# Up projection: the halo's low halves move into the first term, sixteen matmuls of 256 columns follow each other, and the hand-over into the projection is put in another order

## The chip, the cores and the metric

The kernel runs on one core of one Trainium2 chip. Its time is the device time of one execution in microseconds (us). Three runs of the kernel before gave 1258.06, 1258.51 and 1260.97 us; the median is 1258.51. The engines are named as in the profile: PE (TensorE: matmuls, and PEld for the loads of their stationary operand), DVE (VectorE), ACT (ScalarE), POOL (GpSimd) and SP (SyncE, which here issues most DMAs).

## The reference, cut to what matters

The kernel computes one layer of a decoder on 1024 tokens and 16 prepended meta tokens, all in float32: a normalised input, a first projection, a convolution branch and an attention branch that are gated and merged, an output projection with a residual and a layer norm, and then a ConvFFN. The change lies in the up half of that ConvFFN and at the hand-over into it:

```
D_MODEL = 1024
SEQ = 1024
D_FF = 2816
FFN_TAPS = 3

def hybrid_layer(...):
    ...
    h = layer_norm(DEEPNORM_ALPHA * h + mixed @ w_out, ln1_g, ln1_b)
    up = causal_dwconv(h @ ffn_w_up, ffn_dw, ffn_dw_b)
    u, g = jnp.split(up, 2, axis=-1)
    f = (jax.nn.gelu(g, approximate=False) * u) @ ffn_w_down
    return layer_norm(DEEPNORM_ALPHA * h + f, ln2_g, ln2_b)
```

`h @ ffn_w_up` is a product of 1026 rows (1024 tokens and two before them, which the causal convolution of three taps needs) with a matrix of 1024 x 5632.

## The kernel before

**Precision.** A float32 operand x is kept as two rounded parts, hi = round(x) and lo = round(x - hi). A product a x b is then three matmuls, a_hi b_hi + a_hi b_lo + a_lo b_hi, which accumulate in PSUM. The weights are the stationary side (`ah`, `al`), the tokens the moving side.

**Seven products for eight.** The up projection is cut into 22 chunks. For each, a 2 x 2 arrangement of blocks (the two halves of the features of h, by the two halves of the tokens; the two halves of the outputs) is computed by seven block products in place of eight. In the order of the loop they are named `B11`, `B21`, `BT2`, `BT4`, `BT1`, `BT3`, `B22` after their token operand. `B11`, `B21` and `B22` are blocks of h itself, the four `BT` are differences of such blocks, formed on DVE (`form_t2`, `form_t3`, `form_t4`). The weight side of each product is a raw block or a sum of raw blocks, formed per chunk on DVE (L1411), rounded to its high half on ACT (L1393) and subtracted to its low half on DVE (L1394). These halves lie in a ring of ten places, so they are made ahead of use.

**Columns.** A half of the tokens has 514 columns: 2 of halo (the two tokens ahead of it) and 512. It is cut into two parts, part 0 with 258 columns (halo and 256) and part 1 with 256. Each product goes over 4 blocks of 128 features with 3 terms: 12 matmuls of 258 columns for part 0, and then 12 of 256 columns for part 1, in the order features outside, terms inside (L1572). Part 0 ends at the end of one PSUM bank, part 1 begins the next.

**PSUM.** Four tiles of two banks each are used in turn: X (`px`), Z (`pz`), V4 (`pw`) and Y (`py`). The products go to X, Z, X, V4, Y, X, Y. Between them ACT copies X and Y out (`copy`, L1584) and DVE combines (`tt`, L1580) into the four blocks c11, c21, c22, c12. For each of those, `conv_ffn` does the three taps: the first on ACT (L1499), two more on DVE (L1500, L1501); gelu runs on ACT (L1505), gate times value on DVE (L1509), and the result goes to DRAM.

**The hand-over.** Ahead of the up projection stands the output projection (`out_rows`: PSUM tiles `ps_w`, added to the residual on DVE in L1327, normalised in L1351), one block of 128 tokens after another, the last of them block 5. Its rows have to be transposed on PE (`turn`, L1361) and scaled on ACT (L1374) before the operands of part 0 can be formed. For this reason chunk 0 goes in two passes: part 1 first, and after its third product the transposes of block 5, in the banks of V4 and Z; then part 0. While part 1 runs, DVE and ACT make the operands of part 0: `form_t2` and the others (L1273), high halves on ACT (L1264), low halves on DVE (L1269).

**What sets the order.** The loop is written in the order above. A scheduler then puts each engine's instructions into one fixed row, by rank and by the orders that `after` adds; `line` chains the DVE work of the hand-over one behind the other in the order of the text. On the chip each engine takes its row in order and waits for semaphores. The lines that matter below:

```
        if pinned_w[0]:
            line(ins)
        elif ring_next[0] <= 10:
            after(ins, formed[0])
...
                    for k in range(4):
                        ks = slice(k * P, (k + 1) * P)
                        for j, (x, hl) in enumerate(((ah, 0), (ah, 1), (al, 0))):
                            ins = nc.tensor.matmul(o, x[:, ks], bmat(sub, q, hl, k), ...)
```

Of the kernel before, what the change touches and what calls it, by code (L numbers as in the profile page):

```python
# [58 lines left out]

HW = 514  # L60
SUB = [(0, 258), (258, HW)]

W_LEN = 2304

# [48 lines left out]
def tile_hybrid_layer(  # L113
# [1113 lines left out]
    def quadrant(sub, kk, h):  # L1227
        i = h * KC + kk * 4
        return FA[:, h1_at(sub, i):h1_at(sub, i + 4)]

    B_AT = [[(RHC, 40), (RHO, 4096 + 40)] + [(OA, OA_UP + i * KC * BS[0]) for i in range(4)] + [(RX, 56)],
            [(OC, OC_UP + i * 2048) for i in range(4)] + [(RHC, 4096 + R_DN), (RHC, 2048 + R_DN), (RHC, 6144 + R_DN)]]
    B11, B21, BT2, BT1, BT3, BT4, B22 = range(7)

    def bsum(sub, q, hl):
        n, s = SUB[sub][1] - SUB[sub][0], BS[sub]
        t, o = B_AT[sub][q]
        return t[:, o + hl * 4 * s:o + (hl + 1) * 4 * s].rearrange("p (k n) -> p k n", k=4)[:, :, :n]

    def bmat(sub, q, hl, k):  # L1240
        return bsum(sub, q, hl)[:, k]

    lined, high = [], []

# [14 lines left out]

    def bsplit(sub, q, src, cs=slice(None)):  # L1260
        with rank(RK_SUMS):
            hi, lo = (bsum(sub, q, hl)[:, :, cs] for hl in range(2))
            src = wide(src)[:, :, cs]
            ins = nc.scalar.copy(hi, src)  # L1264
# [4 lines left out]
            line(nc.vector.tensor_tensor(lo, src, f32(hi), OP.subtract))  # L1269

    def bsub(out, x, y, cs=slice(None)):
        with rank(RK_SUMS):
# [83 lines left out]
    def turn(i, r, n, ins, banks=None, behind=None, upper=False):  # L1356
        with rank(RK_TURN):
            for j, k0 in enumerate((4, 0) if upper else (0, 4)):
                ps = banks[j] if banks else pat.tile([P, 512], F, name="ps_h", tag="s", bufs=2)
                for k in range(4):  # L1360
                    ins = nc.tensor.transpose(ps[:, k * P:(k + 1) * P], r[:, (k0 + k) * P:(k0 + k + 1) * P], ident)  # L1361
                    if behind:
                        after(ins, behind[-1])
                        behind.append(ins)
                for k in range(k0, k0 + 4):
                    src = ps[:, (k - k0) * P:(k - k0) * P + n]
                    if n < P:
                        dst = edge[:, 0, k]
                    else:
                        h, jj = divmod(i, 4)  # L1370
                        sub = 0 if jj < 2 else 1
                        a = 2 + jj * P - SUB[sub][0]
                        dst = h1F(sub, h, k)[:, a:a + P]
                    nc.scalar.activation(dst, src, AF.Identity, bias=b1col(k), scale=g1col(k))  # L1374
# [10 lines left out]
    def wsplit(src):  # L1385
        i = ring_next[0]
        ring_next[0] += 1
        i %= len(RING)
        if RING[i] is None:
            RING[i:i + 2] = wsp_flat()  # L1390
        t = RING[i]
        hi, lo = t[:, 0:512], t[:, 512:1024]
        nc.scalar.copy(hi, src)  # L1393
        ins = nc.vector.tensor_tensor(lo, src, f32(hi), OP.subtract)  # L1394
        if pinned_w[0]:
            line(ins)
        elif ring_next[0] <= 10:
            after(ins, formed[0])
        return hi, lo

    def w_rows(c):
# [89 lines left out]
        ft_next[0] += 1  # L1491
        return FA[:, i * 512:(i + 1) * 512]

    c11, c21, u2 = (FA[:, 4128 + i * HW:4128 + (i + 1) * HW] for i in range(3))
    c12, c22, u13 = (RT[:, i * HW:(i + 1) * HW] for i in range(3))

    def conv_ffn(cc, o):
        t = ftmp()
        nc.scalar.activation(t, cc[:, 2:HW], AF.Identity, bias=ffw(3, o), scale=ffw(2, o))  # L1499
        nc.vector.scalar_tensor_tensor(t, cc[:, 1:HW - 1], ffw(1, o), t, OP.mult, OP.add)  # L1500
        nc.vector.scalar_tensor_tensor(t, cc[:, 0:HW - 2], ffw(0, o), t, OP.mult, OP.add)  # L1501
        return t
# [42 lines left out]
            load((td if i < FH else sd)[j, :, h * 1024:(h + 1) * 1024], t[h])  # L1545

    last_mm, copied = [], []
    w_first(7)
    pinned_w[0] = False
    for c in range(FC):  # L1550
        V4, X, Z, Y = (pup.tile([P, 1024], F, name=n, tag=n) for n in ("pw", "px", "pz", "py"))
        passes = ((1,), (0,)) if c == 0 else ((0, 1),)
        for subs in passes:
            last = subs == passes[-1]
            w_next = iter(range(7))
            a, b = SUB[subs[0]][0], SUB[subs[-1]][1]

            def at(t):
                return t[:, 254 + a:254 + b]

            def prod(q, bank, first):
                if last:
# [2 lines left out]
                else:  # L1565
                    ah, al = w_ready[next(w_next)]
                for sub in subs:
                    o = bank[:, 254 + SUB[sub][0]:254 + SUB[sub][1]]
                    for k in range(4):
                        ks = slice(k * P, (k + 1) * P)  # L1570
                        for j, (x, hl) in enumerate(((ah, 0), (ah, 1), (al, 0))):
                            ins = nc.tensor.matmul(o, x[:, ks], bmat(sub, q, hl, k), start=first and k + j == 0,  # L1572
                                                   stop=k == 3 and j == 2, skip_group_check=not first)
# [11 lines left out]

            prod(B11, X, True)
            copy(u13[:, a:b], at(X))
            prod(B21, Z, True)
            if last and c not in (0, FH + 1):
                sums_load(c - 1 if c <= FH else c - 2)  # L1590
# [13 lines left out]
            if last:  # L1604
                g0 = gelu(conv_ffn(c11, FC + c))
            prod(BT4, V4, True)
# [2 lines left out]
            prod(BT3, X, False)  # L1609
            copy(u13[:, a:b], at(X))  # L1610
            ins = tt(c22[:, a:b], c22[:, a:b], u13[:, a:b], OP.add)
            if last and c not in (0, FH + 1):
                sums_form(c - 1 if c <= FH else c - 2, ins)
            tt(c21[:, a:b], u13[:, a:b], at(V4), OP.subtract)
            prod(B22, Y, False)
            tt(c12[:, a:b], at(Y), u2[:, a:b], OP.add)
            if last:
                f1 = conv_ffn(c22, c)
                f_out(c, 0, g0, conv_ffn(c21, c))
# [9 lines left out]
    D8 = [pdn.tile([P, 512], F, name="ps_" + "xxzzzzxx"[j], tag=f"d{j}") for j in range(8)]  # L1629
    X, Z = ([D8[j] for j in b] for b in ((0, 1, 6, 7), (4, 5, 2, 3)))  # L1630


    def blk(t, first, step, col):
# [237 lines left out]
```

## Time and profile before

| What | Value |
|---|---|
| Runs | 1258.06, 1258.51, 1260.97 us (median 1258.51) |
| Profiled execution | 1258.79 us, its span 1257.0 us |
| Mean granted PE clock | 0.998 |
| Up projection on PE | from 602.92 to 1039.27 us of the span |
| of it the first pass of chunk 0 (part 1) | 602.92 to 615.23 us |
| of it the second pass of chunk 0 (part 0) | 615.23 to 625.66 us |
| one later chunk | 19.7 us |

Times in the profile are counted from the first instruction. In the timeline a row gives the start, the time from there to the end of the last instruction of the row, the engine, the line, the operation, the tile written and the tiles read, the shape, and how many follow each other; in brackets stands how long the engine had stood idle before, and what ended it. On PE the ends of matmuls are modelled and overlap: their spacing is read from the starts. In the chain of waits a row gives the start, the length and what ran.

### The profile page before, as it was taken

How to read it: one execution, taken by the hardware profiler on the slowest of the kernel's cores; microseconds unless marked ns; L12 is line 12 of the kernel's file. 1: busy time of each engine (PE TensorE's matmuls, PEld its weight loads, DVE VectorE, ACT ScalarE, POOL GpSimd, SP SyncE). 2: the span in 40 equal slices, each digit the busy share in tenths (PEclk: the TensorE clock that was granted, in tenths of full speed). 3: DMA queues.
4: the chain of work that ended last, by engine and by line, in shares of the span. 5: the costliest groups of instructions: out<-in, count | busy, mean ns of one | idle time of the engine just before them, and what ended most of it. 6: DMA issues, size and time to landing. Idle time of an engine off the chain costs nothing.

```text
span 1257.0 us, 23022 instructions
## 1 busy us (share of the span) xinstructions
PE 1243.3 (99%) x9176; PEld 1178.3 (94%) x9176; DVE 1076.1 (86%) x1855; ACT 597.1 (48%) x1108; POOL 7.4 (1%) x8
## 2 busy tenths in 40 slices
PE   9999999999999999999999999999999999999997
PEld 8999999999999999788899999999999998888886
DVE  8989999999978677548899999998989977896697
ACT  8433264655474233344655555455555544445330
POOL 0000000001000000000000000000000000000000
PEclk9999999999999999999999999999999999999999
DMA  6393633422256554222145545454454566998712
GB/s 260 118 299 102 186 89 104 116 81 85 73 156 187 168 154 110 84 101 85 51 171 199 190 177 205 162 207 149 157 199 160 199 226 251 394 346 334 276 60 84
DMA packets 98685, 212.19 MB, mean 169 GB/s; under 512 B 11395, under 2 KB 38595, under 8 KB 98322
## 3 DMA queue, kind: packets, MB, share of 16 engines
q1 hardware_dynamic: 84414, 199.57, 46.6%
q10 hardware_dynamic: 14164, 11.15, 2.8%
q8 instruction: 72, 1.18, 0.4%
q14 instruction: 35, 0.29, 0.1%
HBM read 150.29 MB, written 62.70 MB: 169 GB/s over the span
## 4 chain that ended last, share of the span: by engine, by line
PE 96%; DVE 2%; ACT 1%; DMA 0%; issue 0%; DVEq 0%; SPq 0%; ACTq 0%
PE px L1572 15%; PE py L1572 10%; PE ps_x L1717 9%; PE ps_z L339 8%; PE ps_z L342 8%; PE ps_z L343 8%; PE ps_z L1717 7%; PE ps_p L1171 7%; PE pz L1572 5%; PE pw L1572 5%; PE ps_w L343 2%; PE ps_w L342 2%; PE ps_w L339 2%; PE ps_z L574 2%; PE ps_t L942 1%; PE ps_s L918 1%
## 5 line engine op out<-in xcount | busy, mean ns | idle before, releaser
L339 PE MATMUL ps_z<-RHO,w 128*128 128x256 f32 (+2 forms) x864 | 243.3, 282 | 0.0
L342 PE MATMUL ps_z<-RHO,w 128*128 128x256 f32 (+2 forms) x864 | 242.5, 281 | 0.0
L343 PE MATMUL ps_z<-RHC,w 128*128 128x256 f32 (+2 forms) x864 | 242.4, 281 | 0.0
L342 PEld LDWEIGHTS ps_z<-RHO,w 128*128 128x128 f32 x864 | 162.5, 188 | 0.5
L343 PEld LDWEIGHTS ps_z<-RHC,w 128*128 128x128 f32 x864 | 162.8, 188 | 0.2
L339 PEld LDWEIGHTS ps_z<-RHO,w 128*128 128x128 f32 x864 | 162.6, 188 | 0.1
L748 DVE SCALAR_TENSOR_TENSOR FA<-cin,cdw,FA 128x1026 f32<-128x1026 f32 x120 | 154.5, 1297 | 0.7
L1394 DVE TENSOR_TENSOR RHO<-wr,RHO 128x512 fp32r<-128x512 f32 x94 | 64.1, 690 | 8.0 <-ACT RHO L1393 7.9
L299 ACT CAST w<-wr 128x1024 fp32r<-128x1024 f32 x37 | 38.8, 1048 | 63.4 <-PE ps_z L343 49.9
L1393 ACT CAST RHO<-wr 128x512 fp32r<-128x512 f32 x94 | 56.9, 620 | 24.6 <-DVE wr L1411 12.4
L1411 DVE TENSOR_TENSOR wr<-wr 128x512 f32<-128x512 f32 x88 | 60.8, 691 | 0.1
L757 ACT ACTIVATE FA<-ps_z,colr 128x258 f32<-128x258 f32 (+1 forms) x64 | 30.1, 472 | 60.1 <-PE ps_z L343 52.5
L302 DVE TENSOR_TENSOR w<-wr,w 128x1024 fp32r<-128x1024 f32 x37 | 45.1, 1218 | 8.1 <-ACT w L299 7.9
L1584 ACT COPY FA<-px 128x514 f32<-128x514 f32 (+2 forms) x23 | 13.2, 573 | 78.7 <-PE px L1572 78.7
L1171 PE MATMUL ps_p<-OC,w 128*128 128x256 f32 (+1 forms) x384 | 48.1, 278 | 0.0
L1171 PE MATMUL ps_p<-OA,w 128*128 128x256 f32 (+1 forms) x384 | 47.8, 278 | 0.0
L1171 PEld LDWEIGHTS ps_p<-OC,w 128*128 128x128 f32 x384 | 46.2, 188 | 0.1
L1171 PEld LDWEIGHTS ps_p<-OA,w 128*128 128x128 f32 x384 | 45.9, 188 | 0.0
L1394 DVE TENSOR_TENSOR w<-wr,w 128x512 fp32r<-128x512 f32 x60 | 40.9, 690 | 5.7 <-ACT w L1393 5.6
L1572 PE MATMUL px<-OA,RHO 128*128 128x258 f32 x324 | 43.2, 282 | 0.0
L1499 ACT ACTIVATE FA<-OB,coll 128x512 f32<-128x512 f32 x44 | 35.9, 815 | 14.9 <-DVE OB L1580 14.9
L1572 PE MATMUL px<-OC,RHO 128*128 128x256 f32 x324 | 41.5, 277 | 0.8 <-DVE OB L1327 0.8
(450 smaller groups left out, 3082.0 us busy)
## 6 DMA issues: line engine op xcount, KB each, us to landing
wr<-in_w_up_dram SPq DMA_DIRECT2D x44, 512.0 KB, 3.6
wr<-in_w_z_dram SPq DMA_DIRECT2D x29, 512.0 KB, 4.1
OB<-in_w_down_dram SPq DMA_DIRECT2D x24, 512.0 KB, 4.8
fd<-FA SPq DMA_DIRECT2D x44, 256.0 KB, 2.0
FA<-sd SPq DMA_DIRECT2D x15, 512.0 KB, 8.9
qt<-qd SPq DMA_DIRECT2D x28, 256.0 KB, 4.3
OB<-td SPq DMA_DIRECT2D x14, 512.0 KB, 8.9
sgd<-FA ACTq DMA_DIRECT2D x48, 128.0 KB, 2.7
```

What stands on the lines that cost most here:

```text
L299: ins = nc.scalar.copy(hi, raw)
L302: return nc.vector.tensor_tensor(lo, raw, f32(hi), OP.subtract)
L339: ins = nc.tensor.matmul(ps, al, bh, start=i == 0, stop=False)
L342: nc.tensor.matmul(ps, ah, bh, start=False, stop=False)
L343: last = nc.tensor.matmul(ps, ah, bl, start=False, stop=i == n - 1)
L748: nc.vector.scalar_tensor_tensor(acc[c], cin[:, j:j + U], wc, acc[c], OP.mult, OP.add)
L1171: nc.tensor.matmul(ps[:, :b - a], x, rhs(k, hl, a, b), start=k + j == 0, stop=k == 3 and j == 2)
L1393: nc.scalar.copy(hi, src)
L1394: ins = nc.vector.tensor_tensor(lo, src, f32(hi), OP.subtract)
L1411: ins = nc.vector.tensor_tensor(*x)
L1572: ins = nc.tensor.matmul(o, x[:, ks], bmat(sub, q, hl, k), start=first and k + j == 0, stop=k == 3 and j == 2, skip_group_check=not first)
L1717: nc.tensor.matmul(banks[i], l[:, ts], r[:, ws], start=first and a and x + k == 0, stop=z and x == len(ops) - 1 and k == 2, skip_group_che ...
```

## The change

**Terms of a product.** The operand rows of part 0 get another layout. A high row now has a stride of 264 columns: 2 columns with the low half of the halo, 2 with its high half, 256 with the high halves. The low row keeps only the 256. The first term (`ah` times the high row) takes 260 columns, the term with `al` 258, the term with the low row 256, and they now go term by term: four matmuls of 260, four of 258, four of 256, and then part 1 with its twelve of 256. The product of the halo's low half therefore lands in two columns of its own, is carried through copies and sums (516 columns in place of 514), and is added by two operations of one column each on ACT at the start of every `conv_ffn`.

**Low halves of part 0.** Each is now two operations on DVE: one for the 256 columns, a small one for the halo.

**PSUM banks.** Y takes banks 0 and 1, V4 2 and 3, Z 4 and 5, X 6 and 7 (before: V4, X, Z, Y). The transposes of block 5 go to Y and Z in place of V4 and Z. The last stage's names are changed so that its X and Z are again the banks of `pw`, `py` and of `pz`, `px`.

**Hand-over.** Block 5's second four transposes are evacuated on DVE (L1393 of the changed kernel) and not on ACT. On DVE the later columns of `B11` and `B21` get their low halves before that evacuation; the low halves of the seventh weight operand come behind it, and those of the following chunk's first three behind all token operands. Some orders between copies, casts and sums of chunk 0 are added.

What this does to the rows of the engines is seen at three places. In all of them the lines of the changed kernel carry other numbers: L1599 is the matmul (before L1572), L1379 the transposes (L1361), L1415 the weights' low halves (L1394), L1433 their sums (L1411), L1607 the sums behind the products (L1580), L1611 the copies (L1584), L1414 the casts (L1393), L1524 to L1526 the taps (L1499 to L1501), L1530 gelu (L1505), L1534 gate times value (L1509), and L1522 the new halo additions.

PE at the beginning of the up projection, before:

```order
L1572 MATMUL px<-OC,RHO 128x256 x12
L1572 MATMUL pz<-OC,RHO 128x256 x12
L1572 MATMUL px<-OC,RHO 128x256 x12
L1361 MATMUL pw<-coll,OB 128x128 x4
L1361 MATMUL pz<-coll,OB 128x128 x4
L1572 MATMUL pw<-RHC,RHO 128x256 x12
L1572 MATMUL py<-OC,w 128x256 x12
L1572 MATMUL px<-RHC,w 128x256 x12
L1572 MATMUL py<-RHC,w 128x256 x12
L1572 MATMUL px<-RHC,RHO 128x258 x12
L1572 MATMUL pz<-RHO 128x258 x12
```

and PE at the same place in the changed kernel:

```order
L1599 MATMUL px<-OC,RHO 128x256 x12
L1599 MATMUL pz<-OC,RHO 128x256 x12
L1599 MATMUL px<-OC,RHO 128x256 x12
L1379 MATMUL py<-coll,OB 128x128 x4
L1379 MATMUL pz<-coll,OB 128x128 x4
L1599 MATMUL pw<-RHC,RHO 128x256 x12
L1599 MATMUL py<-OC,w 128x256 x12
L1599 MATMUL px<-RHC,w 128x256 x12
L1599 MATMUL py<-RHC,w 128x256 x12
L1599 MATMUL px<-RHC,RHO 128x260 x4
L1599 MATMUL px<-RHC,RHO 128x258 x4
L1599 MATMUL px<-RHC,RHO 128x256 x4
```

The order of the products is the same; the first transposes write `py`, which is next used two products later and not at once, and every product of part 0 is three groups of four.

DVE around the boundary of chunk 0 and chunk 1, before. The rows L1394 are, in this order, the low halves of chunk 1's weights for `BT3`, `BT2` and `B22` (that for `BT1` stands six rows above the first):

```order
L1394 TENSOR_TENSOR RHO<-wr,RHO 128x512
L1411 TENSOR_TENSOR wr<-wr 128x512
L1501 SCALAR_TENSOR_TENSOR FA<-FA,coll 128x512
L1394 TENSOR_TENSOR RHO<-wr,RHO 128x512
L1500 SCALAR_TENSOR_TENSOR FA<-OB,coll,FA 128x512
L1500 SCALAR_TENSOR_TENSOR FA<-FA,coll 128x512
L1500 SCALAR_TENSOR_TENSOR FA<-OB,coll,FA 128x512
L1394 TENSOR_TENSOR RHO<-wr,RHO 128x512
L1501 SCALAR_TENSOR_TENSOR FA<-OB,coll,FA 128x512
L1580 TENSOR_TENSOR FA<-pz,OB 128x514
```

and in the changed kernel, where the rows L1415 are the low halves for `BT1`, `BT3` and `BT2`:

```order
L1433 TENSOR_TENSOR wr<-wr 128x512
L1525 SCALAR_TENSOR_TENSOR FA<-FA,coll 128x512
L1526 SCALAR_TENSOR_TENSOR FA<-OB,coll,FA 128x512
L1433 TENSOR_TENSOR wr<-wr 128x512
L1525 SCALAR_TENSOR_TENSOR FA<-OB,coll,FA 128x512
L1526 SCALAR_TENSOR_TENSOR FA<-FA,coll 128x512
L1415 TENSOR_TENSOR RHO<-wr,RHO 128x512
L1607 TENSOR_TENSOR FA<-pz,OB 128x516
L1415 TENSOR_TENSOR RHO<-wr,RHO 128x512
L1526 SCALAR_TENSOR_TENSOR FA<-OB,coll,FA 128x512
L1415 TENSOR_TENSOR RHO<-wr,RHO 128x512
L1534 TENSOR_TENSOR FA<-FA 128x512
```

The low half for `BT2`, the third product of chunk 1, stood ahead of most taps of chunk 0 and of the first sum of chunk 1 (L1580 with 514 columns); now it stands behind all eight taps of chunk 0, behind that sum (L1607 with 516 columns), and behind the low halves of two later products.

ACT in the middle of the projection, at the end of one chunk, before:

```order
L1584 COPY OB<-px 128x514
L1393 CAST RHO<-wr 128x512
L1393 CAST w<-wr 128x512
L1499 ACTIVATE FA<-OB,coll 128x512
L1499 ACTIVATE FA<-FA,coll 128x512
L1499 ACTIVATE FA<-OB,coll 128x512
L1584 COPY OB<-px 128x514
```

and in the changed kernel:

```order
L1611 COPY OB<-px 128x516
L1414 CAST RHO<-wr 128x512
L1414 CAST w<-wr 128x512
L1522 ACTIVATE OB<-OB 128x1 x2
L1524 ACTIVATE FA<-OB,coll 128x512
L1522 ACTIVATE FA<-FA 128x1 x2
L1524 ACTIVATE FA<-FA,coll 128x512
L1522 ACTIVATE OB<-OB 128x1
L1611 COPY OB<-px 128x516
L1522 ACTIVATE OB<-OB 128x1
L1524 ACTIVATE FA<-OB,coll 128x512
```

Two one-column operations now stand ahead of each first tap; here the copy of the next chunk's first product has moved between them. In SP's row the loads of raw weights of chunk 2 and later move behind one or two stores of chunk 0 and by such a step in places later on; POOL's row is the same.

The diff, cut to its core:

```diff
+CU = HW + 2
...
-    B_AT = [[(RHC, 40), (RHO, 4096 + 40)] + [(OA, OA_UP + i * KC * BS[0]) for i in range(4)] + [(RX, 56)],
-            [(OC, OC_UP + i * 2048) for i in range(4)] + [(RHC, 4096 + R_DN), (RHC, 2048 + R_DN), (RHC, 6144 + R_DN)]]
+    HP = 264
+    B_AT = [[(RHC, 16, 0), (RHO, 4096 + 16, 0)] + [(OA, 8 + i * 2080, i % 2) for i in range(4)] + [(RX, 32, 0)],
+            [(OC, OC_UP + i * 2048, 0) for i in range(4)] + [(RHC, x + R_DN, 0) for x in (4096, 2048, 6144)]]
...
+    def bmat(sub, q, j, k):
+
+        if sub:
+            return row(1, q, j % 2)[:, k]
+        return row(0, q, j % 2)[:, k, (0, 0, 2)[j]:(260, 256, 260)[j]]
...
-            line(nc.vector.tensor_tensor(lo, src, f32(hi), OP.subtract))
+            n = src.shape[2]
+            a = cs.start or 0
+            x = 2 if sub == 0 and a == 0 else 0
+            a -= 2 if sub == 0 and a else 0
+            lo = bsum(sub, q, 1)[:, :, a:a + n - x]
+            line(nc.vector.tensor_tensor(lo, src[:, :, x:], f32(hi)[:, :, x:], OP.subtract))
+            if x:
+                line(nc.vector.tensor_tensor(row(0, q, 0)[:, :, 0:2], src[:, :, :2], f32(hi)[:, :, :2], OP.subtract))
...
-                    nc.scalar.activation(dst, src, AF.Identity, bias=b1col(k), scale=g1col(k))
+                    if upper and j:
+                        line(nc.vector.tensor_scalar(dst, src, g1col(k), b1col(k), OP.mult, OP.add))
+                    else:
+                        nc.scalar.activation(dst, src, AF.Identity, bias=b1col(k), scale=g1col(k))
...
         elif ring_next[0] <= 10:
-            after(ins, formed[0])
+            after(cast, high[-1])
+            after(ins, formed[ring_next[0] - 8])
...
     def conv_ffn(cc, o):
         t = ftmp()
+        for i in range(2):
+            nc.scalar.activation(cc[:, 2 + i:3 + i], cc[:, 2 + i:3 + i], AF.Identity, bias=cc[:, i:i + 1], scale=1.0)
+        cc = cc[:, 2:]
...
-    w_first(7)
-    pinned_w[0] = False
+    w_first(6)
+    for q in (B11, B21):
+        split_of(0, q, LATE)
     for c in range(FC):
-        V4, X, Z, Y = (pup.tile([P, 1024], F, name=n, tag=n) for n in ("pw", "px", "pz", "py"))
+        Y, V4, Z, X = (pup.tile([P, 1024], F, name=n, tag=n) for n in ("py", "pw", "pz", "px"))
...
                 for sub in subs:
-                    o = bank[:, 254 + SUB[sub][0]:254 + SUB[sub][1]]
-                    for k in range(4):
-                        ks = slice(k * P, (k + 1) * P)
-                        for j, (x, hl) in enumerate(((ah, 0), (ah, 1), (al, 0))):
-                            ins = nc.tensor.matmul(o, x[:, ks], bmat(sub, q, hl, k), start=first and k + j == 0,
-                                                   stop=k == 3 and j == 2, skip_group_check=not first)
-                            if k + j == 0 and last_mm:
-                                after(ins, last_mm[-1])
+                    terms = [(k, j) for k in range(4) for j in range(3)]
+                    if sub == 0:
+                        terms = [(k, j) for j in (0, 2, 1) for k in range(4)]
+                    for i, (k, j) in enumerate(terms):
+                        o = bank[:, 512:768] if sub else bank[:, (252, 256, 254)[j]:512]
+                        ins = nc.tensor.matmul(o, (ah, ah, al)[j][:, k * P:(k + 1) * P], bmat(sub, q, j, k),
+                                               start=first and i == 0, stop=i == 11, skip_group_check=not first)
+                        if i == 0 and last_mm:
+                            after(ins, last_mm[-1])
...
             if not last:
-                turn(5, *last_rows, (V4, Z), last_mm, True)
-                for q in (B11, B21):
-                    split_of(0, q, LATE)
+                turn(5, *last_rows, (Y, Z), last_mm, True)
+                w_first(7)
+                pinned_w[0] = False
                 form_t2(0, LATE)
-                formed.append(lined[-1])
                 form_t4(0, LATE)
                 form_t3(0, LATE)
                 for q in (BT2, BT4, BT1, BT3, B22):
                     split_of(0, q)
+                    formed.append(lined[-1])
+                t2_low = formed[0]
+                formed[:2] = []
```

More of the change, by code (lines that the diff above doesn't have):

```diff
@@ L1261, in bsplit @@
         with rank(RK_SUMS):
-            hi, lo = (bsum(sub, q, hl)[:, :, cs] for hl in range(2))
             src = wide(src)[:, :, cs]
+            hi = bsum(sub, q, 0)[:, :, cs]
             ins = nc.scalar.copy(hi, src)
@@ L1587, in tile_hybrid_layer @@
             copy(u13[:, a:b], at(X))
+            if last and c == 0:
+                after(high[-2], copied[-1])
             prod(B21, Z, True)
@@ L1611, in tile_hybrid_layer @@
             ins = tt(c22[:, a:b], c22[:, a:b], u13[:, a:b], OP.add)
+            if not last:
+                after(ins, t2_low)
             if last and c not in (0, FH + 1):
                 sums_form(c - 1 if c <= FH else c - 2, ins)
-            tt(c21[:, a:b], u13[:, a:b], at(V4), OP.subtract)
+            x = tt(c21[:, a:b], u13[:, a:b], at(V4), OP.subtract)
+            if not last:
+                after(x, ins)
             prod(B22, Y, False)
-            tt(c12[:, a:b], at(Y), u2[:, a:b], OP.add)
+            x = tt(c12[:, a:b], at(Y), u2[:, a:b], OP.add)
+            if not last:
+                after(x, ins)
             if last:
```

27 lines of the change are left out of this document (15 added, 12 removed).

## The prediction

> **What bounds the kernel now.** I read the page's totals and the chain of waits first, then the chunks of the up projection one by one, and last the timeline around the hand-over. The page's busy times and its chain by engine:
>
> ```profile
> PE 1243.3 (99%) x9176; PEld 1178.3 (94%) x9176; DVE 1076.1 (86%) x1855; ACT 597.1 (48%) x1108; POOL 7.4 (1%) x8
> ...
> PE 96%; DVE 2%; ACT 1%; DMA 0%; issue 0%; DVEq 0%; SPq 0%; ACTq 0%
> ```
>
> PE has work nearly all the time and holds 96% of the chain, so a shorter row of matmuls shortens the kernel as long as no other engine becomes late. Three later chunks (stretch, sum, then busy time of PE, PEld, DVE, ACT and POOL, granted clock, DMA):
>
> ```profile
> 645.40:665.10 19.70, 19.70 (x171) 19.70 (x170) 18.56 (x31) 10.47 (x19) 0.00 (x0) 1.00 0.55 188
> 665.10:684.80 19.70, 19.70 (x171) 19.70 (x170) 18.25 (x31) 10.26 (x18) 0.00 (x0) 1.00 0.50 188
> 684.80:704.50 19.70, 19.70 (x171) 19.70 (x170) 18.62 (x31) 10.54 (x18) 0.00 (x0) 1.00 0.55 199
> ```
>
> A chunk is limited by PE; DVE has only 1.1 to 1.45 us to spare in it, ACT over 9. DVE is therefore the engine that can take a gain away.
>
> **The saving per product.** Three steps of the chain of waits (start, length): twelve matmuls of 256 columns, twelve of 258, and both together.
>
> ```profile
> 604.55 1.36 PE pz L1572 x12
> ...
> 621.49 1.45 PE py L1572 x12
> ...
> 665.26 2.81 PE px L1572 x24
> ```
>
> One of 256 columns takes 1.36/12 = 113.3 ns, one of 258 takes 1.45/12 = 120.8 ns: 7.5 ns for two columns. What 260 takes is not in the trace. The nearest rows are an earlier stage's 24 matmuls of 272 columns, from the first of them to the matmul behind the last, and the stage with 512 columns:
>
> ```profile
> 53.99 0.29 PE L339 MATMUL ps_z<-RHO,w 128*128 128x272 f32 x1
> ...
> 57.02 0.28 PE L339 MATMUL ps_z<-RHO,w 128*128 128x256 f32 x1
> ...
> 1061.05 8.32 PE L1717 MATMUL ps_z<-RHC,RHO 128*128 128x512 f32 x36
> ```
>
> (57.02 - 53.99)/24 is 126 ns, and 8.32/36 = 231 ns is, with its tail, twice a matmul of 256. So there is a step just above 256, and from 258 to 272 only 5.2 ns in 14 columns, 0.37 per column: 260 takes about 121.5 ns. Bounds: 120.8 (as 258) and 126 (as 272). The change leaves the sum of columns as it was (4 x 260 + 4 x 258 + 4 x 256 = 12 x 258), but takes four of twelve matmuls below the step. Part 0 becomes 4 x 121.5 + 4 x 120.8 + 4 x 113.3 = 1422 ns in place of 1450; a pair saves 27 ns (bounds 10 and 30). The order by terms is taken at nothing: PE loads a stationary operand for each matmul before (9176 loads to 9176 matmuls) and does so after. The Trainium skill, page "TensorE: Matmul & The Clock Gate", section "Back-to-back issue gap", gives a lone matmul N/2.4 + 2.5 ns, which has no step: by it the pair would save nothing, and the 7.5 ns above speak against it.
>
> **The hand-over on PE.** PE's timeline there before (in brackets, idle time and what ended it):
>
> ```profile
> 601.75 0.39 PE L343 MATMUL ps_w<-RW,RHO 128*128 128x512 f32 x1
> 602.92 1.63 PE L1572 MATMUL px<-OC,RHO 128*128 128x256 f32 x12 [0.78 <-DVE OB L1327]
> ...
> 607.11 0.60 PE L1361 MATMUL pw<-coll,OB 128*128 128x128 f32 x4
> 607.55 0.60 PE L1361 MATMUL pz<-coll,OB 128*128 128x128 f32 x4
> ...
> 609.31 1.63 PE L1572 MATMUL pw<-RHC,RHO 128*128 128x256 f32 x12 [1.16 <-ACT FA L1374]
> ...
> 625.66 1.60 PE L1572 MATMUL px<-RHC,w 128*128 128x258 f32 x12
> ...
> 631.34 1.60 PE L1572 MATMUL px<-OA,RHO 128*128 128x258 f32 x12
> ```
>
> The row at 625.66 is chunk 1's first product, that at 631.34 its third (`BT2`). Both waits go: X is now in banks 6 and 7, away from the last `ps_w`, and V4 no longer takes the transposes. The first product can start at 601.75 + 0.23 = 601.98. Seven products of 1.36, the transposes at 2 x 0.44, and 0.25 for the second transposes, which still need `pz` emptied by DVE (my estimate from DVE's row at 606.31 below), put part 0 at 612.63. Seven passes of 1.422 bring chunk 1 to 622.58, 3.1 us earlier than 625.66, and its `BT2` to 622.58 + 2 x (1.422 + 1.36) = 628.15. The low half of its weights is first read by the fifth matmul, at 628.63.
>
> **What is late there.** DVE's rows around the hand-over before:
>
> ```profile
> 605.70 0.69 DVE L1394 TENSOR_TENSOR w<-wr,w 128x512 fp32r<-128x512 f32 x1
> 606.31 0.42 DVE L1580 TENSOR_TENSOR FA<-pz,OB 128x256 f32<-128x256 f32 x1
> ...
> 611.61 0.69 DVE L1273 TENSOR_TENSOR FA<-FA 128x512 f32<-128x512 f32 x1
> 612.33 0.69 DVE L1273 TENSOR_TENSOR OB<-FA 128x512 f32<-128x512 f32 x1
> ...
> 615.35 1.23 DVE L1269 TENSOR_TENSOR OA<-OB,OA 128x1032 fp32r<-128x1032 f32 x1
> 616.49 0.69 DVE L1394 TENSOR_TENSOR RHO<-wr,RHO 128x512 fp32r<-128x512 f32 x1
> 617.09 0.42 DVE L1580 TENSOR_TENSOR OB<-py,FA 128x256 f32<-128x256 f32 x1
> 617.43 0.42 DVE L1580 TENSOR_TENSOR OB<-OB 128x256 f32<-128x256 f32 x1
> ...
> 625.40 0.75 DVE L1500 SCALAR_TENSOR_TENSOR FA<-FA,coll 128x512 f32<-128x512 f32 x1
> 626.07 0.43 DVE L1580 TENSOR_TENSOR OB<-OB 128x258 f32<-128x258 f32 x1
> ...
> 628.93 0.70 DVE L1394 TENSOR_TENSOR RHO<-wr,RHO 128x512 fp32r<-128x512 f32 x1
> ```
>
> Before, the last row shown is the low half for chunk 1's `BT2`: ready at 629.6, 1.7 us ahead of its product. In the changed row it stands behind all taps of chunk 0. I add up that row from the low half at 605.70 to it, each kind by the distance from its start to the next:
>
> - 20 operations of 512 columns (nine low halves of weights, four weight sums, two low halves of `B11` and `B21`, four differences, the sum of 516 columns) at 0.605: 12.1
> - 8 taps at 0.67 (625.40 to 626.07): 5.4
> - 7 sums of 256 or 260 columns and one more at 0.33 to 0.34 (617.09 to 617.43): 2.7
> - 5 low halves of part 0 at 1.14 (615.35 to 616.49): 5.7
> - 5 for the halo, 8 columns each, at 0.11, and the four evacuations of block 5's transposes of 128 columns at 0.2. The nearest rows are a copy of 16 columns, below, and the 0.34 above; they bound the evacuation, and I take a value between them: 1.35 together.
>
> ```profile
> 585.06 0.16 DVE L1453 COPY FA<-edge 128x16 f32<-128x16 f32 x1
> 585.17 0.69 DVE L1328 BATCH_NORM_STATS2 st<-OB 128x6 f32<-128x512 f32 x1
> ```
>
> With the 0.12 that a dependent neighbour adds (611.61 to 612.33, less 0.605) twice, and a tail of 0.09 (0.69 less 0.605), the low half is ready at 605.70 + 27.5 = 633.2. PE, there at 628.63, stands for 4.6 us. Queued behind its fifth matmul are all further products, so the whole of it counts. `BT2` then runs as if it had begun at 632.7 (633.2 less its first four matmuls), 1.4 us later than 631.34 before: what the hand-over gains is more than lost. Bounds: with 0.11 for each evacuation 0.4 less; with two more waits of DVE for ACT of the size that PE had (1.16) 2.3 more.
>
> **The clock.** Nowhere before does PE stand so long between matmuls, save at the end of the kernel (PE's last row; then windows as above, the granted clock third from the right):
>
> ```profile
> 1248.05 0.84 PE L1717 MATMUL ps_x<-RHO 128*128 128x512 f32 x3
> ...
> 1250.00:1251.00 1.00, 0.00 (x0) 0.00 (x0) 0.93 (x3) 0.29 (x1) 0.00 (x0) 1.00 0.61 234
> 1251.00:1252.00 1.00, 0.00 (x0) 0.00 (x0) 1.00 (x3) 0.00 (x0) 0.00 (x0) 0.90 0.00 0
> 1252.00:1253.00 1.00, 0.00 (x0) 0.00 (x0) 0.90 (x5) 0.00 (x0) 0.00 (x0) 0.50 0.00 0
> ```
>
> The last matmul ends at 1248.89. A mean of 0.90 over 1251 to 1252 puts the fall to half at 1251.8, 2.9 us later. A wait of 4.6 us therefore likely halves the clock. How soon it returns the trace doesn't show; if as fast as it fell, PE runs 2.9 us at half speed and loses 1.45. I take 1.4, with 0 (no fall) and twice that as bounds. The Trainium skill, page "TensorE: Matmul & The Clock Gate", section "What's actually happening", speaks against this change: windows of about 3.4 us, idle or busy, switch the clock. By it the loss would be 1.7 us.
>
> **The rest.** 145 pairs follow (5 in chunk 1, 20 chunks of 7): 145 x 27.2 ns = 3.9 us less, with bounds 1.5 and 4.4. ACT's eight additions of one column per chunk, at 0.275 by the row below (2.2/8), are 2.2 us against 9.2 idle: nothing, as long as what needs them is not late (a rival). That ACT no longer evacuates four transposes only helps it. SP's loads of raw weights move behind one or two stores of 2.0 us; they land in 3.6 and are issued about a chunk ahead: nothing. POOL's row is unchanged. The renamed banks of the last stage are the same banks: nothing.
>
> ```profile
> L1374 ACT ACTIVATE edge<-ps_h,colr 128x2 f32<-128x2 f32 x8 | 2.2, 352 | 3.5 <-PE ps_h L1361 3.5
> ...
> wr<-in_w_up_dram SPq DMA_DIRECT2D x44, 512.0 KB, 3.6
> ...
> fd<-FA SPq DMA_DIRECT2D x44, 256.0 KB, 2.0
> ```
>
> The sum: +1.4 (hand-over) + 1.4 (clock) - 3.9 (pairs) = -1.1 us. The profiled execution took 1258.79, 0.28 above the median of the runs; put on the median this is 1257.4. From the bounds: -1.1 - 0.4 - 1.4 - 0.5 = -3.4 to -1.1 + 2.3 + 1.4 + 2.4 = +5.0 if all fell on one side; I keep 1255.1 to 1260.0 for this case.
>
> **Rivals.** *The low half is not late* (faster). If DVE is quicker by some four us, or PE later, `BT2` starts at 628.15, 3.2 us before 631.34, the clock stays, and with the pairs that is -7.1: 1251.4. For it speaks that most of DVE's durations are upper values; against it, the count of its rows. It decides from a wait of about 3 us: then the clock stays too, and -1.1 - 1.4 - 1.6 passes -3.8.
>
> *The pairs save nothing*, since the step comes from another thing than the count of columns, say where in a bank a matmul begins. Then the hand-over and the clock are left: +2.8, 1261.3; without the clock's fall 1259.9. For it: the trace has no 256 beside 258 in one bank; against it, 272 shows the same step.
>
> *DVE becomes the limit of each chunk* (slower). A new chunk on PE has 19.70 - 7 x 0.027 = 19.51 us, DVE is busy for 18.25 to 18.62. Each of four chains copy, additions, first tap, taps grows by 0.55 on ACT. If DVE stands for 1.6 to 2.2 us of this in each chunk, less the 0.9 it has, 0.7 to 1.3 us are lost in 20 chunks: 14 to 26 us, 1271 to 1283. It decides from 0.25 us lost per chunk, that is 1.15 uncovered. Against it: the order puts weight sums and low halves between the sums and the taps, and ACT's queue has over 9 us free.
>
> **How the numbers follow.** About 0.3%, 3.8 us, is what a measurement of this kernel can tell from no change. Main case 0.57, within it. The low half in time: 0.26, faster. No saving by pairs: 0.06, within. DVE the limit: 0.11, slower. Faster 0.26, same 0.63, slower 0.11. The range reaches from a little under the faster rival, 1250.9, to 1260.0, and leaves out the slower rival and the edges, 0.2 in all.
>
> **What would show it.** Right: no wait at the first product nor at V4's first; in chunk 1 a wait of 3.5 to 5.5 us of PE for the weights' low half, and nothing like it later; windows behind it with a granted clock under 1; a chunk of 19.5 us; part 0's groups at about 121, 121 and 113 ns. Wrong: a chunk of 19.7 us or more, PE waits in every chunk, or no wait in chunk 1.

## The result and the profile after

The changed kernel takes 1261.79 us (median of 8 runs, 1261.60 to 1264.37), the kernel before 1258.49 beside it (8 runs). The ratio is 1.0026, with a 95% interval of 1.0017 to 1.0034: 3.3 us slower, inside the 0.3% that I called no change, but outside my range, which ended at 1260.0, and on the other side of the 1.1 us less that I had forecast. My bounds taken together had reached 5.0 us more; the upper end of 1260.0 was a choice of mine within them. The profiled execution took 1261.69, its span is 1259.9 (before 1257.0).

PE's timeline of the changed kernel, at the places shown of before (start, length, engine, line, what; in brackets idle time and what ended it):

```profile
601.77 1.58 PE L1599 MATMUL px<-OC,RHO 128*128 128x256 f32 x12
603.18 1.58 PE L1599 MATMUL pz<-OC,RHO 128*128 128x256 f32 x12
604.59 1.58 PE L1599 MATMUL px<-OC,RHO 128*128 128x256 f32 x12
...
612.52 1.59 PE L1599 MATMUL px<-RHC,RHO 128*128 128x260 f32 x12
...
622.94 1.59 PE L1599 MATMUL px<-RHC,w 128*128 128x260 f32 x12
...
627.21 1.52 PE L1599 MATMUL pz<-OC,RHO 128*128 128x256 f32 x12
631.05 1.23 PE L1599 MATMUL px<-OA,RHO 128*128 128x260 f32 x4 [2.32 <-ACT RHO L1414]
633.24 2.08 PE L1599 MATMUL px<-OA,RHO 128*128 128x258 f32 x8 [0.95 <-DVE RHO L1415]
635.12 2.69 PE L1599 MATMUL px<-OC,RHO 128*128 128x256 f32 x12
637.65 1.59 PE L1599 MATMUL pw<-OA,RHO 128*128 128x260 f32 x12
```

Both waits of before are gone, and PE runs from the projection to chunk 1's second product without a wait that the profile shows. Then it stands twice at chunk 1's `BT2`. The rows of ACT and DVE that end the two waits:

```profile
629.88 1.12 ACT L1414 CAST RHO<-wr 128x512 fp32r<-128x512 f32 x2
...
632.50 0.69 DVE L1415 TENSOR_TENSOR RHO<-wr,RHO 128x512 fp32r<-128x512 f32 x1
```

The granted clock around it (third number from the right):

```profile
630.00:631.00 1.00, 0.00 (x0) 0.00 (x0) 1.00 (x3) 1.00 (x2) 0.00 (x0) 0.89 0.00 0
631.00:632.00 1.00, 0.95 (x4) 0.93 (x4) 1.00 (x3) 0.65 (x3) 0.00 (x0) 0.50 0.00 0
...
637.00:638.00 1.00, 1.00 (x8) 1.00 (x7) 0.00 (x0) 0.00 (x0) 0.00 (x0) 0.70 1.02 262
```

The means of 0.89 and 0.70 put the fall to half at 630.8 and the return at 637.6. The twelve matmuls from 635.12 to 637.65 came at 211 ns.

The chain of waits, one chunk in the middle (`B11`, `B21`, `BT2`, `BT4`, `BT1`, `BT3`, `B22`), where every step was 2.81 before:

```profile
688.34 2.84 PE px L1599 x24
691.17 2.79 PE pz L1599 x24
693.96 2.84 PE px L1599 x24
696.80 2.80 PE pw L1599 x24
699.60 2.77 PE py L1599 x24
702.38 2.84 PE px L1599 x24
705.22 2.79 PE py L1599 x24
```

I had 2.79 for all of them. X's three products became slower than before, and the seven together take 19.66 to 19.67 us in place of 19.69. The timeline of the last chunk shows where in a product this lies. First the kernel before, `BT2` in X and the beginning of `BT4`, then the changed kernel, `BT2`, `BT4` and the beginning of `BT1`:

```profile
1025.20 1.60 PE L1572 MATMUL px<-OA,RHO 128*128 128x258 f32 x12
1026.63 1.54 PE L1572 MATMUL px<-OC,RHO 128*128 128x256 f32 x12
1028.01 1.61 PE L1572 MATMUL pw<-OA,RHO 128*128 128x258 f32 x12
```

```profile
1028.13 1.59 PE L1599 MATMUL px<-OA,RHO 128*128 128x260 f32 x12
1029.56 1.58 PE L1599 MATMUL px<-OC,RHO 128*128 128x256 f32 x12
1030.97 1.60 PE L1599 MATMUL pw<-OA,RHO 128*128 128x260 f32 x12
1032.41 1.52 PE L1599 MATMUL pw<-RHC,RHO 128*128 128x256 f32 x12
1033.77 1.58 PE L1599 MATMUL py<-OA,RHO 128*128 128x260 f32 x12
```

In the changed kernel, part 1 of X runs from 1029.56 to 1030.97, about 117.5 ns for a matmul of 256 columns; part 1 of V4 from 1032.41 to 1033.77, 113.3 ns. Before, `BT2` split its 2.81 into 1.43 and 1.38, and so did `BT3`, while the other five took the 1.45 and 1.36 of the prediction. So the kernel before already had two prices for either width. The first pass of chunk 0 shows the same pair of values for the very same matmuls on the same operands: 1.41 to 1.42 per product at 601.77, 603.18 and 604.59 here, where PE came without a pause from the projection; 1.36 in the kernel before, where it had stood idle for 0.78 us. The bank does not explain it: the product in `pz` lies in banks 4 and 5 both times. So a matmul of 256 columns has two steady spacings here, and in this pass the stream keeps the one that it came in with.

PE's first row of the last stage, before and then in the changed kernel, closes the account:

```profile
1039.27 5.63 PE L1717 MATMUL ps_z<-OC,RHC 128*128 128x512 f32 x24
```

```profile
1042.17 5.63 PE L1754 MATMUL ps_z<-OC,RHC 128*128 128x512 f32 x24
```

The up projection ends 2.90 us later. Chunk 1's fourth product begins at 637.65, before at 631.34 + 2.81 = 634.15: the hand-over lost 3.5. From there to the end it is 404.52 us in place of 405.12: the pairs gave 0.6.

### The profile page after: what moved, and what is told of

Read it like the earlier page. It is cut to its first block, busy times and chain, and to the rows that moved or that the text cites. A ratio compares the mean times of both kernels' runs of the same rounds, so it can differ in the third digit from the quotient of the medians.

```text
span 1259.9 us, 23195 instructions
## 1 busy us (share of the span) xinstructions
PE 1244.9 (99%) x9176; PEld 1180.0 (94%) x9176; DVE 1079.3 (86%) x1866; ACT 626.1 (50%) x1280; POOL 7.4 (1%) x8
## 4 chain that ended last, share of the span: by engine, by line
PE 94%; DVE 4%; DMA 0%; ACT 0%; issue 0%; DVEq 0%; SPq 0%
PE px L1599 14%; PE py L1599 9%; PE ps_x L1754 9%; PE ps_z L340 8%; PE ps_z L343 8%; PE ps_z L344 8%; PE ps_z L1754 7%; PE ps_p L1172 7%; PE pw L1599 5%; PE pz L1599 4%; PE ps_w L344 2%; PE ps_w L343 2%; PE ps_w L340 2%; PE ps_z L575 2%; PE ps_t L943 1%; PE ps_s L919 1%
## 5 line engine op out<-in xcount | busy, mean ns | idle before, releaser
L1415 DVE TENSOR_TENSOR RHO<-wr,RHO 128x512 fp32r<-128x512 f32 x94 | 63.8, 684 | 4.3 <-ACT RHO L1414 4.2
L1414 ACT CAST RHO<-wr 128x512 fp32r<-128x512 f32 x94 | 56.8, 618 | 15.5 <-DVE wr L1433 7.1
L1433 DVE TENSOR_TENSOR wr<-wr 128x512 f32<-128x512 f32 x88 | 60.0, 682 | 0.2
L1611 ACT COPY FA<-px 128x516 f32<-128x516 f32 (+2 forms) x23 | 13.1, 570 | 70.9 <-PE px L1599 70.9
L1599 PE MATMUL px<-OA,RHO 128*128 128x260 f32 (+1 forms) x324 | 44.6, 287 | 3.3 <-ACT RHO L1414 2.3
L1415 DVE TENSOR_TENSOR w<-wr,w 128x512 fp32r<-128x512 f32 x60 | 40.7, 684 | 8.2 <-ACT w L1414 8.1
L1599 PEld LDWEIGHTS px<-OA,RHO 128*128 128x128 f32 x324 | 41.5, 193 | 3.8 <-ACT RHO L1414 2.5
L1599 PE MATMUL px<-OC,RHO 128*128 128x256 f32 x324 | 43.7, 286 | 0.0
```

What stands on the lines that cost most here:

```text
L1414: cast = nc.scalar.copy(hi, src)
L1433: ins = nc.vector.tensor_tensor(*x)
L1599: ins = nc.tensor.matmul(o, (ah, ah, al)[j][:, k * P:(k + 1) * P], bmat(sub, q, j, k), start=first and i == 0, stop=i == 11, skip_group_ch ...
```

## The experiments

Two things had to be explained: the hand-over (3.5 us lost, where I had 2.8) and the pairs (0.6 gained, where I had 3.9). For the pairs the first theories were: the place of X in PSUM; the order by terms; what ran before a product, together with where its operand rows lie. Times of a product and of a chunk are the distances between starts, the same to 1 or 2 ns from chunk 3 on. Where no interval is given, the time is that of one run, and the chain carries the verdict.

**The low half in time.** Chunk 0's taps wait for chunk 1's low half for `BT2`:

```diff
+        if ring_next[0] == 11:
+            bt2_low.append(ins)
...
-        nc.vector.scalar_tensor_tensor(t, cc[:, 1:HW - 1], ffw(1, o), t, OP.mult, OP.add)
+        ins = nc.vector.scalar_tensor_tensor(t, cc[:, 1:HW - 1], ffw(1, o), t, OP.mult, OP.add)
+        if o in (0, FC) and bt2_low:
+            after(ins, bt2_low[0])
```

> The changed kernel, but chunk 0's taps on DVE wait until chunk 1's weights for BT2 have their low half. Theory (the hand-over is lost to that low half and to the clock that falls behind the wait): no wait of PE at chunk 1's third product, granted clock 1.00 throughout the hand-over, chunk 1's fourth product at about 631.4 us where the changed kernel has 637.65, so about 6 us faster than the changed kernel: 1255.5. Chunks 2 and later keep 19.67 us. Rival (ACT's cast of the high half is what is late, and ACT's row is not moved): PE still waits 1 to 2.3 us there, the clock may stay, 1257.5 to 1260.

Measured: 1256.60 us (10 runs; ratio to the kernel before 0.9980, interval 0.9970 to 0.9989), 5.2 less than the changed kernel by the medians. Its PE at the same place, and the window with the granted clock:

```profile
628.79 0.64 PE L1603 MATMUL px<-OA,RHO 128*128 128x260 f32 x4
629.69 1.22 PE L1603 MATMUL px<-OA,RHO 128*128 128x258 f32 x8 [0.26 <-DVE RHO L1415]
...
632.16 1.58 PE L1603 MATMUL pw<-OA,RHO 128*128 128x260 f32 x12
```

```profile
626.00:630.00 4.00, 3.74 (x32) 3.53 (x31) 2.86 (x5) 3.26 (x6) 0.00 (x0) 1.00 0.01 2
```

0.26 us of wait are left, the clock stays at 1.00, and the fourth product begins at 632.16 in place of 637.65. The loss of the hand-over was the order of chunk 0's taps ahead of `BT2`'s weights, and the clock behind the wait. The run does not part DVE's low half from ACT's cast of the high half: the new order also brought that cast forward, to before 628.79, where PE starts `BT2`, from 631.0. Later chunks keep their 19.67, as expected.

**The banks of X and Y exchanged.**

```diff
-        Y, V4, Z, X = (... for n in ("py", "pw", "pz", "px"))
+        X, V4, Z, Y = (... for n in ("px", "pw", "pz", "py"))
```

> The changed kernel with the banks of X and Y exchanged (X in banks 0 and 1, Y in 6 and 7), no order changed. In the changed kernel X's three products take 2.839 us in each chunk, because their matmuls of 256 columns come at 118 ns; those of Z, V4 and Y come at 113. If banks 6 and 7 are what is slow, then X's products fall to about 2.79 and Y's two rise to 2.83 or 2.84: a chunk of 19.6. If it is what ran before a product and where its operands lie (two spacings of the same matmul, and the stream keeps the one that it came in with), X's three stay at 2.839 and the others as they are: 19.67.

Measured: 1263.00 us. The chain, `B11`, `B21` and `BT1`:

```profile
688.71 2.84 PE px L1599 x24
691.55 2.79 PE pz L1599 x24
...
699.97 2.77 PE py L1599 x24
```

All seven steps are as in the changed kernel. The bank is not the cause.

**The order of terms alone, and the terms without their order.** In the kernel before, part 0's twelve matmuls of 258 go term by term; in the changed kernel, its 260, 258 and 256 go block by block:

```diff
-                    for k in range(4):
-                        for j, (x, hl) in enumerate(((ah, 0), (ah, 1), (al, 0))):
...
+                        terms = [(k, j) for j in (0, 2, 1) for k in range(4)]
```

```diff
-                        terms = [(k, j) for j in (0, 2, 1) for k in range(4)]
+                        terms = [(k, j) for k in range(4) for j in (0, 2, 1)]
```

> The kernel before with only the order of part 0's twelve matmuls changed, term by term in place of block by block; all twelve keep 258 columns, nothing is moved on other engines. If the order of terms costs nothing by itself: 2.813 us per product, 19.69 per chunk, 1258.5. If it is part of what ate the gain (each matmul then has another stationary operand's block after it and another moving row): products up to 2.85, a chunk up to 19.95, 1259 to 1264.

> The changed kernel with part 0's matmuls block by block (260, 258, 256, and again), so that there are no sixteen of 256 in a row at its end. If the width alone sets a matmul's time, as my prediction took it, 2.787 in place of the 2.813 before, whatever the order. If the sixteen in a row matter: 2.81 or more for each product, 19.7 or more per chunk. If X's slow part 1 comes from how part 0 ends, X's three products change here while Z's and Y's may too.

Measured: 1260.93 and 1264.23 us. The chains of waits, `B21` and `BT2` of the first, `BT2` and `BT4` of the second:

```profile
688.49 2.83 PE pz L1573 x24
691.31 2.81 PE px L1573 x24
```

```profile
694.64 2.83 PE px L1599 x24
697.48 2.80 PE pw L1599 x24
```

With nothing but the order changed, five of the seven products of the kernel before take 2.83 in place of 2.81, and a chunk 19.76. The widths in block order, with the rows at their new addresses, take 2.83 or 2.80, a chunk 19.77. The prices do not add up: each alone costs 0.07 us per chunk, and both together gain 0.03. The price belongs to the whole sequence. The starts of the single matmuls show where it is paid: in the slower products of both runs part 1 begins with three to six matmuls that mostly take 118 to 125 ns, and then goes over to 113.

**Only the address of the rows.** In the changed kernel `BT1` and `BT4` have their low row ahead of the high one. Once all seven got the high row first, once all the low row; every engine's order stays the same up to a few rows in the last stage.

```diff
-    B_AT = [[(RHC, 16, 0), (RHO, 4096 + 16, 0)] + [(OA, 8 + i * 2080, i % 2) for i in range(4)] + [(RX, 32, 0)],
+    B_AT = [[(RHC, 16, 0), (RHO, 4096 + 16, 0)] + [(OA, 8 + i * 2080, 0) for i in range(4)] + [(RX, 32, 0)],
```

```diff
+    B_AT = [[(RHC, 16, 1), (RHO, 4096 + 16, 1)] + [(OA, 8 + i * 2080, 1) for i in range(4)] + [(RX, 32, 1)],
```

> The changed kernel with the low row behind the high row for BT1 and BT4 too, as for the other five; nothing but the address of these rows changes. If a product's spacing hangs on the one before it (fast in, slow out; slow in, fast out, for this layout), fast and slow take turns, with seven products to a chunk so that they change places from chunk to chunk: products of 2.84 and 2.79 in turn, a mean chunk of 19.7. If it hangs on the tile X alone, X's three stay at 2.839 and the rest at 2.77 to 2.80: 19.65.

> The changed kernel with the low row ahead of the high row for all seven operands. BT1, the one product that comes after a fast one and stays fast, has this layout (2.773 us). If the layout does this, all seven take 2.77 to 2.80 in every chunk: 19.45, and 20 chunks give 4.4 us less than the changed kernel. If it hangs on the tile X, X's three stay at 2.839 and a chunk at 19.65.

Measured: 1266.61 and 1265.06 us. The chains, `B21` and `BT4` of the first; `BT4`, `BT1`, `BT3` and `B22` of the second:

```profile
691.41 2.85 PE pz L1599 x24
...
697.11 2.85 PE pw L1599 x24
```

```profile
697.63 2.79 PE pw L1599 x24
700.42 2.77 PE py L1599 x24
703.20 2.84 PE px L1599 x24
706.04 2.85 PE py L1599 x24
```

Both theories as I had written them fell: with the high row first, all seven take 2.85 (a chunk 19.93), nothing takes turns; with the low row first, `BT4` and `BT1` alone stay fast. But the address matters, with all else equal. By the addresses of the built kernels, in the changed kernel and in the second run here `BT1` and `BT4` are the ones whose high rows and whose low rows both begin at byte 32 of a stretch of 256 bytes (as all rows of part 1 do; the weights begin at 96). This is the place of the first of the four blocks; the others of a high row follow 1056 bytes apart, those of a low row 1024. In the changed kernel the high rows of the other five begin at 160, in the second run here both of theirs; in the first run one of the two does for each of the seven.

**One more matmul ahead of X's part 1.** It has 64 columns and writes to the bank in which X accumulates, so that X's sums are no longer those of the layer; the number and shape of all other instructions stay, and only the times are used.

```diff
+                        if sub == 0 and i == 11 and bank is X and c > 1:
+                            nc.tensor.matmul(bank[:, 960:1024], al[:, 384:512], bmat(1, q, 0, 0)[:, 0:64],
+                                             start=True, stop=True, skip_group_check=True)
```

> The changed kernel with one more matmul, of 64 columns into an unused place of the tile, between part 0 and part 1 of each of X's three products from chunk 2 on. If X's part 1 is slow only because of the moment at which its stream of 256 begins, it falls to 113 ns per matmul after it: 12 x 4.4 ns = 53 less against 30 to 60 for the added one, X at 2.79 to 2.85 with 113 in its later matmuls, and Z's, V4's and Y's products may change with it. If X's tile or operands are slow as such, 118 stays and X takes 2.87 to 2.90.

Measured: 1270.77 us. The chain, `B21`, and further on the two parts of `BT3`:

```profile
692.65 2.85 PE pz L1599 x24
...
704.03 1.43 PE px L1599 x12
705.49 1.46 PE px L1599 x12
```

In `BT3`, part 1 behind the added matmul takes 1.46: by the starts of the single matmuls its first takes 199 ns, the next three 116 to 122, and from the fifth on they come at 113. In `B11` and `BT2` they stay at 118. `B21`, to which nothing was done, went from 2.79 to 2.85. So a product hangs on what ran before it; the expectation that an added matmul would free all three of X's products failed.

**Six operands at the place of `BT1`.** On top of the first experiment:

```diff
-    B_AT = [[(RHC, 16, 0), (RHO, 4096 + 16, 0)] + [(OA, 8 + i * 2080, i % 2) for i in range(4)] + [(RX, 32, 0)],
+    B_AT = [[(RHC, 48, 1), (RHO, 4096 + 48, 1), (OA, 8, 0)] + [(OA, 2088 + i * 2112, 1) for i in range(3)] + [(RX, 0, 1)],
```

(The tile `OA` grows by 16 columns; `BT2` stays where it was.)

> The kernel of e1 (chunk 1's low half for BT2 in time) with other addresses for part 0's operands: six of the seven now have both rows at the same place within 256 bytes as BT1 has in the changed kernel (2.773 us there), all with the low row ahead; BT2 keeps high ahead of low, with its high rows 128 bytes off, as in the changed kernel. Theory (the place of the rows sets the spacing): six products at 2.77 to 2.80, BT2 at 2.80 to 2.84, a chunk of 19.45 to 19.55 in place of 19.67, so 2.5 to 4.5 us less than e1 (its median 1256.6): 1252 to 1254. Rival (the spacing hangs on what ran before in a way that the place doesn't tell): some products at 2.84 to 2.85 again, a chunk of 19.6 to 19.9, 1255 to 1261.

Measured: 1254.22 us (6 runs), ratio to the kernel before 0.9965, interval 0.9952 to 0.9977. The chain, `BT2`, `BT4`, `BT1`, `BT3`:

```profile
688.27 2.84 PE px L1603 x24
691.11 2.80 PE pw L1603 x24
693.91 2.77 PE py L1603 x24
696.68 2.77 PE px L1603 x24
```

Five products take 2.77, `BT4` behind the slow `BT2` 2.80, `BT2` 2.84: a chunk of 19.51. By the interval this kernel is faster than the one before, and its chunks are 0.19 us shorter than there: 27 ns per product, the very saving that I had forecast for a pair, but as a mean of five times 40, 12 and -26.

**One operand moved.** The last two runs take the changed kernel and move the rows of `B11` alone, once with the low row ahead, once with the high row ahead and 32 columns between them:

```diff
-    B_AT = [[(RHC, 16, 0), ...
+    B_AT = [[(RHC, 48, 1), ...
```

```diff
+    B_AT = [[(RHC, 48, 0), ...
...
-        n = 256 if hl else hi
+        n, o = 256 if hl else hi, o + (32 if (sub, q, hl) == (0, B11, 1) else 0)
```

> The changed kernel with one operand moved: part 0's rows of B11 go 32 columns (128 bytes) further, with the low row ahead of the high, so that both stand within 256 bytes where BT1's stand. Nothing else differs. From what the runs so far show of the two kinds of place and of the product before, I read off all seven: B11 2.773 in place of 2.839; then B21, which now comes after a fast product, 2.839 in place of 2.787; BT2 after a slow one 2.787 in place of 2.839; BT4 after a fast one 2.773 in place of 2.801; BT1 2.773, BT3 2.839, B22 2.787 as they are. A chunk of 19.57. If the products don't hang on the one before: only B11 moves, 19.60; if the place isn't the cause, nothing moves, 19.67.

> As the run before, but B11's high row stays ahead of its low row, with 32 columns between them so that both stand at the same place within 256 bytes. If the place is what counts and not which row is ahead: the same seven times as in the run before, 19.57. If the order of the rows in memory counts: B11 at 2.84 and the others as in the changed kernel, 19.67.

Measured: 1258.90 and 1259.26 us, both with the same seven times. The chain of the first, `B11`, `B21`, `BT2`, `BT4`:

```profile
687.24 2.77 PE px L1599 x24
690.01 2.84 PE pz L1599 x24
692.85 2.79 PE px L1599 x24
695.64 2.77 PE pw L1599 x24
```

All seven came as read off beforehand, and a chunk takes 19.57. Moving one operand by 128 bytes changed four products, three of which weren't touched; which row is ahead does not count. In this sequence a product with both rows at byte 32 goes over to 113 ns in its part 1, whatever came before (2.77 behind a fast product, 2.79 or 2.80 behind a slow one); one with its high rows at byte 160 and its low rows at 32 comes out slow behind a fast product (2.84), and fast behind such a slow one (2.79).

## Why the prediction was wrong

**The hand-over was read rightly, and its size nearly.** In time order, forecast and measured: first product 601.98, 601.77; part 0 at 612.63, 612.52; chunk 1 at 622.58, 622.94; its `BT2` without a wait at 628.15, and 627.21 + 1.36 = 628.57; the low half ready at 633.2, and 632.50 + 0.69 = 633.19. That PE stood there already for the high half (ACT's cast, which ended at 631.0) changes nothing in the end, since the low half came later. The clock fell, as I took as likelier, 2.1 us after PE's last matmul had ended at 627.21 + 1.52. It stayed at half for 6.8 us, of which PE worked through 20 matmuls from 633.24 to 637.65; at 119 and 117.5 ns these take 2.4, so 2.0 us were lost. I had 1.4, the bounds 0 and 2.8. This term was mis-sized by 0.6; the rest of the hand-over, 3.5 less 2.0, came to 1.5, where I had 1.4. Nor is the clock's term fixed: of the seven other runs that keep these waits, three stayed at half clock for 6.8 us and four for 3.4. The Trainium skill, page "TensorE: Matmul & The Clock Gate", section "What's actually happening", has windows of about 3.4 us for the switch. One or two such windows at half clock agree with it; the fall, after 2.1 us of idle time and so less than one window, does not.

**The step that failed is "145 pairs follow: 145 x 27.2 ns = 3.9 us less".** The chunks gave 0.6. The working under it took the time of a matmul as a function of its columns, 113.3 for 256 and 120.8 for 258, and my bounds of 10 and 30 ns varied only the price of 260. That price was not what failed: in X's `B11` the four of 260 came at 118.8 ns, under my 121.5, but the four of 256 behind them at 117 and part 1 at 117.8. Over the seven products part 0 became 18 ns shorter in the mean, where I had 27, and part 1, for which I had put no change, 15 ns longer. Measured from start to start, the pairs of `B21`, `BT4`, `BT1` and `B22` save 26, 12, 40 and 26 ns, and X's three lose 26 each: 4 ns in the mean. The 113.3 was no price of 256 columns but one of two spacings; the other is about 117.5. The new addresses of the rows had no term in my sum at all, and the order by terms was taken at nothing; alone, it costs the kernel before 0.07 us per chunk (19.76 against 19.69).

**The rival that came closest** is that the pairs save nothing, with 1261.3 against 1261.79. That it came so close is in part luck, since its mechanism was only half right. Where in a bank a matmul begins does not make the difference: all seven products begin at the same places of their banks, and take 2.77 to 2.84. What does is where in SBUF the moving rows begin, and in which spacing PE comes in. The Trainium skill, page "TensorE: Matmul & The Clock Gate", section "Back-to-back issue gap", gives a lone matmul one value for each width, by my estimate from it 109.2 ns for 256 columns; the trace has neither 109.2 nor one value. The rival with DVE as the limit fell: chunks take 19.67 with ACT's halo additions in them, and PE waits in none of the later ones.

What stays open is why byte 32 and not 160 lets the stream run at 113 ns, and what in PE or in its reading of SBUF keeps the spacing from one matmul to the next. The runs show the pattern for this sequence of widths and for these addresses of the weights, not a rule for others; and even here the same kind of operand that comes out fast behind a product of 2.84 stayed slow behind one of 2.85, in the run with all high rows first.

## What to carry to other kernels

A time per matmul that is read from one place of a trace holds for that place: its neighbours and the addresses of its rows are part of it. Where a change reorders matmuls or moves their operands, compare the steps of the chain product by product, since here products with the same matmuls took 2.77 to 2.85 us, and try a move of the rows by 128 bytes before giving the change up. Whoever puts an order on low halves at a hand-over should follow the one that is needed first, and count waits like the 2.3 and 1.0 us here with the half clock behind them: it came in all eight runs that have them.

## What the runs showed of the hardware

- A stream of matmuls with 256 columns ran at 113.3 or at 117.5 ns, with the same operands, and kept its spacing over 36 matmuls in a row. An idle time of PE of 0.78 us stood ahead of it in the two runs with 113.3, none in the ten with 117.5.
- Moving one operand's rows by 128 bytes moved its product from 2.84 to 2.77 us and three untouched ones by -52 to +52 ns. With all seven high rows first a chunk took 19.93 us, with six operands at byte 32 it took 19.51: 2.1% of a chunk by addresses.
- Exchanging the PSUM banks of X and Y made no difference: all seven steps were the same.
- The clock halved 2.1 us after PE's last matmul here and took 6.8 us to return, with PE at work for 5.6 of them. In the seven other runs that keep the waits it was back after 6.8 us (three) or 3.4 us (four). At the kernel's end it fell 2.0 to 5.3 us after the last matmul, over all twelve runs.
